# Fourth recurrent head in the wide form, memory's rows normalised in two parts, and two changes to how three streams of work are interleaved

## The chip, the cores and the metric

The kernel runs on one core of a Trainium2 chip. The metric is the device time of one execution in microseconds (us); less is better. The engines are named as in the profile: PE (TensorE matmul), PEld (its weight load), DVE (VectorE), ACT (ScalarE), POOL (GpSimd) and SP (SyncE, which here only issues DMAs). Each runs its own queue of instructions in order, and the engines wait for each other by semaphores.

## What is computed

One encoder layer over 512 tokens of width 1024, in float32. The part that the change touches is the first of three sub-layers. One input projection feeds an attention group of 8 heads and a recurrent group of 4 heads; both results go through one output projection, and then follow a cross-attention into 256 memory tokens and a gated MLP. Of the recurrent group the reference says, cut to its core:

```python
def step(S, xs):                      # chunks of tokens, both directions
    qx, kx, vx, lx = xs
    bcum = jnp.cumsum(lx, axis=-2)
    dec = jnp.exp(jnp.where(tri, bcum[..., :, None, :] - bcum[..., None, :, :], -jnp.inf))
    a = jnp.einsum("...tk,...sk,...tsk->...ts", qx, kx, dec)
    o_intra = jnp.einsum("...ts,...sv->...tv", a, vx)
    o_inter = jnp.einsum("...tk,...kv->...tv", qx * jnp.exp(bcum), S)
    ...
m = rmsnorm(mem, mem_norm_g[l])       # the memory's rows, 256 x 1024
```

## The kernel before

**Shapes.** Every large product is written as three matmuls of rounded float32 (`mm3`, lines 296 to 298: high part by high, high by low, low by high). A unit of weights is 128x1024; ACT rounds it to its high part (L240), and DVE, ACT or POOL make the low part (L242, L247, L245 with a DMA, L248). The eight PSUM banks are four tags, "b", "s", "c" and "o", of two banks each.

**The recurrent heads.** `hgrn_in(h)` projects queries and both directions' forget gates. `hgrn_core(h)` then builds a 512x512 matrix of decayed products level by level, where a level m joins neighbouring blocks of m tokens: ACT copies the keys of a level in order (L682), PE makes four 128x128 products in bank "c" (L685), DVE multiplies queries and keys by the next decay (two L711, one L716) and writes the level's products into the matrix under a mask (L725, a predicated copy). Levels 1 to 64 are done so; 128 and 256 follow with L692, L697 (transposes), L702 (the states' products) and L731 to L733 (the outputs), then ACT sums the squares (L737), POOL makes the root, DVE scales (L745), PE turns the result (L749), and ACT and DVE split it (L143, L144).

**Two forms for the diagonal and level 1.** In the narrow form (head 3, the fourth) ACT makes two copies (L669), PE makes two times four 128x128 float32 products (L672 for the diagonal, L685 with `m == 1`), ACT copies the first into the matrix (L673) and DVE puts the second in under a mask. In the wide form (heads 0 to 2) DVE multiplies queries and keys token by token (L655, L661), both results are split (L139 on ACT, L140 on DVE), and four 128x512 matmuls against a 0/1 matrix `parity` (L722) sum them, after which ACT copies the result (L723).

**How the order of the work is set.** The program is written by interleaved Python generators. `weave` (lines 83 to 105) holds a progress for each stream, as a share of the stream's total, and lets the one that is furthest behind emit its next piece; a piece says how much it counts. `pace(us)` makes a stream yield nothing until the streams together have emitted so many counted us. Nothing waits by `pace` on the chip: it only sets where instructions stand in each engine's queue. A stream that yields nothing keeps its old progress, unless it is listed in `late`:

```python
if step is None and s[0] in late and i + 1 < len(live):
    s[1] = max(s[1], live[i + 1][1] / live[i + 1][2] * s[2])
```

There are two weaves. The first (line 890) runs the projections beside the heads' cores, with `late=(cores,)`. The second (line 996) runs what is left of the cores, `attention()` and `attention_filler()`, without `late`. The attention does 32 steps i: two score matmuls (L921), a softmax (DVE maximum L899, ACT exponential L902, DVE reciprocal L903, a scaling on ACT L907 or DVE L909), four transposes of step i-2 (L931, split by L139 and L140), and every fourth step eight matmuls with the values (L942, then L946 and L947). The filler is the memory's key projection (128x256 matmuls, 192 of them), the first half of its value projection (48 matmuls of 128x512) and the first half of the output projection (96 of 128x512), whose parts after the first wait for all four recurrent heads.

**The memory's rows.** `mem_norm()` (line 844) normalises two blocks of 128 rows between head 1's and head 2's projections: a square on ACT (L344), a root on POOL, two scalings on DVE (L328) for each block.

Of the kernel before, what the change touches and what calls it, by code (L numbers as in the profile page):

```python
# [10 lines left out]
F32R = mybir.dt.float32r  # L11
# [36 lines left out]
NEG_SCALAR = frozenset(range(9, 33))  # L48
NEG_POOL = frozenset(range(33, 42))
CORE_SHARE, ATT_LEAD = 53.0, 4.0  # L50
CORE_WIDE, CORE_END = 8.0, 4.5
KEY_TURNS = {1: (0, 1), 2: (2, 3)}
WARM, SPREAD_STEP = 4, 2
LEVELS = (1, 2, 4, 8, 16, 32, 64)
# [53 lines left out]
def layer(tc, io, out):  # L108
# [23 lines left out]
    def tmp2(shape=(P, 512), dt=F32, tag="ta"):  # L132
        return t2.tile(list(shape), dt, name="tmp2", tag=tag, bufs=TMP_BUFS[tag])

    def tmp4(shape, dt=F32):
        return t4.tile(shape, dt, name="tmp4", tag="tmp4")
# [419 lines left out]
        for b in range(NB):  # L556
            put_v(b, v_ps[b])

    masks = const.tile([P, len(LEVELS), P], U8, name="masks")
    masks_f = tmp4([P, len(LEVELS), P])  # L560
# [4 lines left out]
    with tc.issue_after(last_load[0]):  # L565
        nc.sync.dma_start(lbt, io["hg_lb"])
        nc.sync.dma_start(og, io["hg_out_norm_g"][:, None])
        nc.sync.dma_start(masks_f, io["masks"])
        nc.sync.dma_start(qkg[:, 0, :], rows_bc(io["q_norm_g"], 64))
        nc.sync.dma_start(qkg[:, 1, :], rows_bc(io["k_norm_g"], 64))  # L570
        nc.sync.dma_start(cw, io["conv"])
# [68 lines left out]
    def hgrn_core(h):  # L640
# [6 lines left out]
        kt = room[:, 1024:1536].rearrange("p (s n) -> p s n", s=NB)  # L647
        st = room[:, 1536:1792].rearrange("p (g n) -> p g n", g=2)
        diag = a[:, :, 0, :]
        wide = h < 3  # L650
        near = room[:, 1024:2048]
        ksum = tmp2(tag="th")
        nc.scalar.mul(ksum, qk[:, 1, 0, :], oml[:, 0, h:h + 1])
        if wide:
            nc.vector.tensor_tensor(out=pat(near, T, [[2, T // 2], [1 - T, 2]]), in0=pat(qk, 0, [[2, T // 2], [T + 1, 2]]),  # L655
                                    in1=pat(qk, 3 * T + 1, [[2, T // 2], [-(T + 1), 2]]), op=ALU.mult)
        nc.vector.scalar_tensor_tensor(out=ksum, in0=qk[:, 1, 1, :], scalar=oml[:, 1, h:h + 1], in1=ksum,
                                       op0=ALU.mult, op1=ALU.add)
        if wide:
            pairs = lambda t: t.rearrange("p (i two) -> p i two", two=2)  # L660
            nc.vector.tensor_tensor(out=pat(near, 0, [[2, T // 2], [T + 1, 2]]), in0=pairs(ksum), in1=pairs(q),  # L661
                                    op=ALU.mult)
            sides = [[tmp2(dt=F32R, tag="th") for _ in range(2)] for _ in range(2)]
            for n in range(2):
                split(*sides[n], near[:, n * T:n * T + T])
        else:
            kc, qc = [tmp2(tag="th") for _ in range(2)]
            for side, to in ((1, kc), (0, qc)):
                nc.scalar.copy(to, pat(qk, side * 2 * T, [[2, T // 2], [T + 1, 2]]))  # L669
            o = bank("c").rearrange("p (b n) -> p b n", b=NB)  # L670
            for b in range(NB):
                nc.tensor.matmul(o[:, b, :], ksum[:, blk(b)], q[:, blk(b)], start=True, stop=True)  # L672
            nc.scalar.copy(diag, o)  # L673
            yield 1.0
        toff = 0
        for i, m in enumerate(LEVELS + (128, 256)):
            if m == 1 and wide:
                pass
            elif m <= 64:
                if m > 1:  # L680
                    kc = tmp2(tag="th")
                    nc.scalar.copy(kc, pat(qk, 2 * T, [[2 * m, T // (2 * m)], [T + m, 2], [1, m]]))  # L682
                o = bank("c").rearrange("p (b n) -> p b n", b=NB)
                for b in range(NB):
                    nc.tensor.matmul(o[:, b, :], kc[:, blk(b)], qc[:, blk(b)] if m == 1 else  # L685
                                     pat(qk, b * P, [[2 * m, P // (2 * m)], [T + m, 2], [1, m]]),
                                     start=True, stop=True)
            elif m == 128:
                o = bank("c").rearrange("p (b n) -> p b n", b=NB)
                for sb in range(NB):  # L690
                    tb = sb ^ 1
                    nc.tensor.matmul(o[:, sb, :], qk[:, 1, sb % 2, blk(sb)], qk[:, 0, tb % 2, blk(tb)],  # L692
                                     start=True, stop=True)
            else:
# [18 lines left out]
            if m < 128:  # L713
                src = tt[:, toff:toff + 2 * nblk].rearrange("p (i two) -> p two i", two=2)
                toff += 2 * nblk
                nc.vector.tensor_mul(tt[:, toff:toff + nblk], src[:, 0, :], src[:, 1, :])  # L716
                if m == 1 and wide:
                    yield from pace(CORE_WIDE)
                    o = bank("c")
                    for n in range(2):  # L720
                        for k in range(2):
                            nc.tensor.matmul(o, parity[:, n:n + P], sides[n][k], start=n + k == 0, stop=n + k == 2)  # L722
                    nc.scalar.copy(diag, o.rearrange("p (b n) -> p b n", b=NB))  # L723
                else:
                    nc.vector.copy_predicated(diag, masks[:, i:i + 1, :].to_broadcast([P, NB, P]), o)  # L725
            else:
                nc.scalar.copy(a[:, :, 1, :], o)
            yield 1.0
# [11 lines left out]
        if wide:  # L740
# [100 lines left out]
        for b in range(MB):  # L841
            nc.scalar.dma_start(kv["rows"][:, b, :], io["mem"][blk(b), :])

    def mem_norm():
        for b in range(MB):
            m = kv["rows"][:, b, :]
            r = row_rstd(m, tmp4([P, D]))
            for c in range(2):
                scale_rows(m, r, kv["g"], m, c)

    def mem_turn(b):
        if b == 0:
# [3 lines left out]
    def mix_projections():  # L856
# [541 lines left out]
```

## Time and profile before

| what | value |
|---|---|
| median of 3 runs | 814.66 us (813.87 to 815.19) |
| the profiled execution's own time | 814.31 us |
| its span, first to last instruction | 812.5 us |
| PE busy | 800.7 us, 99% |
| PE's share of the chain that ended last | 89% |
| PEld busy | 688.4 us, 85% |
| DVE busy | 582.7 us, 72% |
| ACT busy | 482.0 us, 59% |
| POOL busy | 136.5 us, 17% |

Busy time of PE counts from a matmul's start to its modelled end, and the next one starts before that, so the spans of consecutive matmuls overlap: a PE that is busy all the time can still start its matmuls later than it could. The distance from one start to the next tells more. The waits of an engine are put down to the instruction whose semaphore came last.

### The profile page before, as it was taken

The numbers are of one execution on the slowest core, as the hardware profiler recorded it, in microseconds if no ns is written. First come the engines' busy times: TensorE is split into PE (matmuls) and PEld (weight loads), VectorE is DVE, ScalarE is ACT, GpSimd is POOL, SyncE is SP. The second block draws the span as 40 slices with busy tenths as digits, with TensorE's granted clock in tenths as the row PEclk, the third lists the DMA queues.
The fourth block names the chain that finished last, engine by engine and source line by source line (L and its number), as shares of the span: only waits on it lengthen the run. The fifth ranks groups of instructions, "written<-read, shape, count | busy, mean of one in ns | idle before, by whom it ended". The sixth has DMA issues, their size and how long they took to land.

```text
span 812.5 us, 11696 instructions
## 1 busy us (share of the span) xinstructions
PE 800.7 (99%) x4390; PEld 688.4 (85%) x4390; DVE 582.7 (72%) x878; ACT 482.0 (59%) x797; POOL 136.5 (17%) x213
## 2 busy tenths in 40 slices
PE   9999999999999999999999999999999999999996
PEld 7888878899988888888888898899999998888885
DVE  5467576698896765855453767987777788888765
ACT  6675774677978873645443553665555545566651
POOL 0111201334213102301011311211111111000301
PEclk9999999999999999999999999999999999999999
DMA  8596666679777752256634158776765667278842
GB/s 300 198 267 164 137 148 130 146 187 267 206 193 191 186 188 109 86 173 170 167 117 143 33 165 205 161 199 164 187 166 141 160 187 179 91 211 277 241 127 104
DMA packets 42458, 139.61 MB, mean 172 GB/s; under 512 B 5281, under 2 KB 6561, under 8 KB 42401
## 3 DMA queue, kind: packets, MB, share of 16 engines
q1 hardware_dynamic: 28944, 97.43, 35.0%
q0 software_dynamic: 12160, 38.54, 26.8%
q10 hardware_dynamic: 1296, 2.89, 1.0%
q8 instruction: 34, 0.56, 0.3%
q14 instruction: 24, 0.19, 0.1%
HBM read 135.17 MB, written 25.17 MB: 197 GB/s over the span
## 4 chain that ended last, share of the span: by engine, by line
PE 89%; DVE 4%; ACT 4%; issue 1%; DMA 1%; POOL 1%; SPq 0%; DVEq 0%; POOLq 0%
PE ps_b L298 9%; PE ps_b L297 9%; PE ps_b L296 9%; PE ps_s L296 7%; PE ps_s L298 7%; PE ps_s L297 7%; PE ps_o L296 5%; PE ps_o L298 5%; PE ps_o L297 5%; PE ps_c L296 4%; PE ps_c L298 4%; PE ps_c L297 4%; PE ps_c L685 2%; PE ps_o L942 1%; PE ps_o L931 1%; PE ps_s L921 1%
## 5 line engine op out<-in xcount | busy, mean ns | idle before, releaser
L240 ACT CAST wh<-raw 128x1024 fp32r<-128x1024 f32 x110 | 113.8, 1036 | 106.9 <-PE ps_b L297 30.2
L242 DVE TENSOR_TENSOR wl<-raw,wh 128x1024 fp32r<-128x1024 f32 (+1 forms) x77 | 92.9, 1209 | 72.5 <-ACT wh L240 72.4
L296 PE MATMUL ps_b<-big,wh 128*128 128x512 f32 (+1 forms) x344 | 122.2, 355 | 0.0
L298 PE MATMUL ps_b<-big,wl 128*128 128x512 f32 (+1 forms) x344 | 120.9, 351 | 0.0
L297 PE MATMUL ps_b<-big,wh 128*128 128x512 f32 (+1 forms) x344 | 120.4, 350 | 0.0
L298 PEld LDWEIGHTS ps_b<-big,wl 128*128 128x128 f32 x344 | 65.0, 189 | 8.7
L297 PEld LDWEIGHTS ps_b<-big,wh 128*128 128x128 f32 x344 | 65.1, 189 | 8.2
L296 PEld LDWEIGHTS ps_b<-big,wh 128*128 128x128 f32 x344 | 65.1, 189 | 8.0
L711 DVE TENSOR_TENSOR big<-big 128x512 f32<-128x512 f32 x64 | 48.3, 769 | 9.2 <-ACT tmp L682 4.8
L296 PE MATMUL ps_s<-wh,big 128*128 128x512 f32 (+1 forms) x140 | 53.5, 383 | 0.1
L297 PE MATMUL ps_s<-wl,big 128*128 128x512 f32 (+1 forms) x140 | 53.2, 380 | 0.0
L298 PE MATMUL ps_s<-wh,big 128*128 128x512 f32 (+1 forms) x140 | 53.0, 379 | 0.0
L248 POOL DMA_DIRECT2D wl<-in_w_dram x33 | 29.4, 890 | 118.7 <-ACT wl L247 105.6
L140 DVE TENSOR_TENSOR big<-ps_o,big 128x512 fp32r<-128x512 f32 x54 | 36.8, 686 | 11.5 <-ACT big L139 11.3
L139 ACT CAST big<-ps_o 128x512 fp32r<-128x512 f32 x54 | 31.8, 589 | 17.0 <-PE ps_o L1047 7.5
L296 PE MATMUL ps_s<-big,wh 128*128 128x256 f32 (+1 forms) x120 | 40.0, 333 | 0.0
L297 PE MATMUL ps_s<-big,wh 128*128 128x256 f32 (+1 forms) x120 | 39.9, 333 | 0.0
L298 PE MATMUL ps_s<-big,wl 128*128 128x256 f32 (+1 forms) x120 | 39.9, 332 | 0.0
L297 PE MATMUL ps_c<-big,wh 128*128 128x256 f32 (+1 forms) x120 | 39.1, 325 | 0.0
L296 PE MATMUL ps_c<-big,wh 128*128 128x256 f32 (+1 forms) x120 | 39.1, 325 | 0.0
L298 PE MATMUL ps_c<-big,wl 128*128 128x256 f32 (+1 forms) x120 | 39.0, 325 | 0.0
L296 PE MATMUL ps_o<-wh,big 128*128 128x512 f32 (+1 forms) x102 | 38.8, 380 | 0.0
(322 smaller groups left out, 2147.1 us busy)
## 6 DMA issues: line engine op xcount, KB each, us to landing
raw<-in_w_dram SPq DMA_DIRECT2D x91, 512.0 KB, 3.4
wl<-in_w_dram POOLq DMA_DIRECT2D x33, 512.0 KB, 6.8
sum_t<-in_wd_dram SPq DMA_DIRECT2D x20, 512.0 KB, 6.0
tmp<-in_wu_dram SPq DMA_DIRECT2D x14, 512.0 KB, 7.3
sum_t<-in_wd_dram POOLq DMA_DIRECT2D x10, 512.0 KB, 8.1
sum_t<-sum_t POOLq DMA_DIRECT2D x10, 512.0 KB, 7.4
big<-sum_t SPq DMA_DIRECT2D x10, 512.0 KB, 4.9
raw<-sum_t SPq DMA_DIRECT2D x10, 512.0 KB, 3.8
```

What stands on the lines that cost most here:

```text
L139: nc.scalar.copy(hi, src)
L140: (eng or nc.vector).tensor_sub(lo, src, hi.bitcast(F32))
L240: nc.scalar.copy(wh, raw)
L242: last_low[0] = nc.vector.tensor_sub(wl[:, :by_dma], raw[:, :by_dma], wh[:, :by_dma].bitcast(F32)).ins
L248: nc.gpsimd.dma_start(wl[:, by_dma:], source(i)[:, by_dma:], accum_op=ALU.add)
L296: nc.tensor.matmul(o, a[0], b[0], start=start, stop=False, skip_group_check=again)
L297: nc.tensor.matmul(o, a[0], b[1], start=False, stop=False, skip_group_check=again)
L298: last_mm[0] = nc.tensor.matmul(o, a[1], b[0], start=False, stop=stop, skip_group_check=again).ins
L685: nc.tensor.matmul(o[:, b, :], kc[:, blk(b)], qc[:, blk(b)] if m == 1 else pat(qk, b * P, [[2 * m, P // (2 * m)], [T + m, 2], [1, m]]), st ...
L711: nc.vector.tensor_tensor(out=c, in0=c, in1=pat(tt, toff + off, [[2, npair], [gap, 2], [0, m]]), op=ALU.mult)
L921: nc.tensor.matmul(s, qT[h // 4][:, h % 4, blk(qb)], kT[:, 2 * (h // 4) + c, :], start=c == 0, stop=c == 1)
L931: nc.tensor.transpose(o[:, c, :], e[:, 0, blk(c)], ident)
```

## The change

Five edits. (1) `wide = h < 3` goes: head 3 takes the wide form too, and with it the two paces that only wide heads had, `CORE_WIDE` before the `parity` matmuls and `CORE_END` before the last scaling. (2) The mask of level 1 is no longer loaded or converted (six masks and not seven). (3) `pace(CORE_COPY)`, 1.2 us of counted work, stands between the transposes of level 256 and the states' products, in every head. (4) `mem_norm` takes one block: block 0 where both stood, block 1 after the first projection of head 2. (5) The second weave gets `late=(cores,)`.

```diff
-CORE_WIDE, CORE_END = 8.0, 4.5
+CORE_WIDE, CORE_COPY, CORE_END = 8.0, 1.2, 4.5
...
-        nc.sync.dma_start(masks_f, io["masks"])
+        nc.sync.dma_start(masks_f, io["masks"][:, 1:, :])
...
-        wide = h < 3
...
-        else:
-            kc, qc = [tmp2(tag="th") for _ in range(2)]
-            for side, to in ((1, kc), (0, qc)):
-                nc.scalar.copy(to, pat(qk, side * 2 * T, [[2, T // 2], [T + 1, 2]]))
-            o = bank("c").rearrange("p (b n) -> p b n", b=NB)
-            for b in range(NB):
-                nc.tensor.matmul(o[:, b, :], ksum[:, blk(b)], q[:, blk(b)], start=True, stop=True)
-            nc.scalar.copy(diag, o)
-            yield 1.0
...
                 nc.scalar.copy(kt, o)
                 yield 0.5
+                yield from pace(CORE_COPY)
                 o = bank("c")[:, :256].rearrange("p (g n) -> p g n", g=2)
...
-                if m == 1 and wide:
+                if m == 1:
                     yield from pace(CORE_WIDE)
...
-        if wide:
-            yield from pace(CORE_END)
+        yield from pace(CORE_END)
...
-        mem_norm()
+        mem_norm(0)
         nothing = lambda: None
-        yield from hgrn_in(2, [nothing] * 3 + [lambda: mem_turn(0), nothing, nothing, lambda: mem_turn(1)])
+        yield from hgrn_in(2, [lambda: mem_norm(1), nothing, nothing, lambda: mem_turn(0), nothing, nothing,
+                               lambda: mem_turn(1)])
...
-    weave((cores, 34.0), (attention(), 46.0), (attention_filler(), 52.0))
+    weave((cores, 34.0), (attention(), 46.0), (attention_filler(), 52.0), late=(cores,))
```

What this does to the queues is shown at three places. In the changed program the line numbers are its own: L905 is L921 of before, L915 is L931, L926 is L942, L733 is L749, L669 is L685, L707 is L722, L883 is L899, L887 is L903, L893 is L909, L931 (on DVE) is L947, L696 is L711 and L710 is L725.

**Head 3's first products on PE.** Before, behind the turn of head 2's result (`ps_c<-ident`):

```order
L749 MATMUL ps_c<-ident,tmp_1868 128x128 x4
L672 MATMUL ps_c<-tmp_1296,tmp_2045 128x128 x4
L921 MATMUL ps_s<-big 128x512 x4
L685 MATMUL ps_c<-tmp_2049,tmp_2048 128x128 x4
L685 MATMUL ps_c<-big,tmp_2135 128x128 x4
```

In the change, 35 rows further down the same queue:

```order
L707 MATMUL ps_c<-tmp_2081,parity 128x512
L298 MATMUL ps_b<-big,wl 128x256
L296 MATMUL ps_b<-big,wh 128x256
L707 MATMUL ps_c<-tmp_2082,parity 128x512
L297 MATMUL ps_b<-big,wh 128x256
L298 MATMUL ps_b<-big,wl 128x256
L296 MATMUL ps_b<-big,wh 128x256
L297 MATMUL ps_b<-big,wh 128x256
L669 MATMUL ps_c<-big,tmp_2263 128x128
```

The first level's products stood at once behind the turn; they now stand after the second score, with 46 of the filler's 128x256 matmuls between the turn and the third score, some of them in between the products.

**DVE in the attention, between two row maxima.** Before, from the maximum of step 8 (whose row comes just above the first of these) to that of step 9:

```order
L140 TENSOR_TENSOR big<-ps_o,big 128x4x128
L903 RECIPROCAL small<-small 128x1
L711 TENSOR_TENSOR big<-big 128x16x2x16
L947 TENSOR_TENSOR tmp_2186<-ps_o,tmp_2186 64x512
L140 TENSOR_TENSOR big<-ps_b,big 128x256
L140 TENSOR_TENSOR big<-ps_o,big 128x4x128
L711 TENSOR_TENSOR big<-big 128x32x2x8
L725 COPY_PREDICATED big<-masks,ps_c 128x4x128
L903 RECIPROCAL small<-small 128x1
L140 TENSOR_TENSOR big<-ps_o,big 128x4x128
L909 TENSOR_SCALAR tmp_2277<-tmp_2277,small 128x512
L140 TENSOR_TENSOR big<-ps_b,big 128x256
```

and then one more L711, one more L725 and the maximum. In the change, the longest such stretch, from step 9's maximum to those of steps 10 and 11:

```order
L140 TENSOR_TENSOR big<-ps_o,big 128x4x128
L931 TENSOR_TENSOR tmp_2199<-ps_o,tmp_2199 64x512
L696 TENSOR_TENSOR big<-big 128x32x2x8 x2
L140 TENSOR_TENSOR big<-ps_o,big 128x4x128
L887 RECIPROCAL small<-small 128x1
L710 COPY_PREDICATED big<-masks,ps_c 128x4x128
L893 TENSOR_SCALAR tmp_2244<-tmp_2244,small 128x512
L140 TENSOR_TENSOR big<-ps_o,big 128x4x128
L887 RECIPROCAL small<-small 128x1
L140 TENSOR_TENSOR big<-ps_o,big 128x4x128
L883 TENSOR_REDUCE small<-ps_s 128x1 x2
```

One level's work stands there and not two half levels, and the levels are spread over more steps of the attention: the last product of head 3's levels (L692) stands ahead of step 13's score before, and ahead of step 17's in the change.

**PE late in the attention.** Before, a step of the plain pattern:

```order
L921 MATMUL ps_s<-big 128x512 x2
L931 MATMUL ps_o<-ident,tmp_2682 128x128 x4
L296 MATMUL ps_b<-wh,big 128x512
L297 MATMUL ps_b<-wl,big 128x512
L298 MATMUL ps_b<-wh,big 128x512
```

(the last three twice) and in the change, from step 21's score on:

```order
L905 MATMUL ps_s<-big 128x512 x2
L915 MATMUL ps_o<-ident,tmp_2697 128x128 x4
L905 MATMUL ps_s<-big 128x512 x2
L733 MATMUL ps_c<-ident,tmp_2738 128x128
L296 MATMUL ps_b<-wh,big 128x512
L297 MATMUL ps_b<-wl,big 128x512
L298 MATMUL ps_b<-wh,big 128x512
L915 MATMUL ps_o<-ident,tmp_2752 128x128 x4
L296 MATMUL ps_b<-wh,big 128x512
L297 MATMUL ps_b<-wl,big 128x512
L298 MATMUL ps_b<-wh,big 128x512
L926 MATMUL ps_o<-big,vv 128x512 x8
```

Between the scores of steps 20 and 28 stand 23 of the filler's matmuls and not 48, because the value projection is used up and the output projection's next part waits for head 3, whose turn (L733) now stands behind step 22's score and not behind step 19's. The 25 others follow, with more, in one block of 31 ahead of step 29's score.

## Rows read from the trace of the kernel before

**Rows 1.** Windows: stretch, length; busy of PE, PEld, DVE, ACT, POOL; granted clock; DMA.

```profile
207.20:256.40 49.20, 47.97 (x328) 42.02 (x327) 42.60 (x82) 41.27 (x84) 12.12 (x13) 1.00 0.78 204
256.40:299.00 42.60, 42.60 (x221) 34.83 (x220) 31.94 (x64) 35.14 (x76) 7.01 (x8) 1.00 0.67 169
```

**Rows 2.** Chain that ended last, 205 to 300 us: start, length, engine, tile, line.

```profile
213.03 1.40 ACT tmp L907 x2
...
232.16 1.13 PE ps_c L685 x8
...
247.30 0.66 PE ps_o L931 x4
```

**Rows 3.** PE's groups by line, 207.4 to 256.4 us: count, busy, mean ns, idle.

```profile
L921 PE MATMUL ps_s<-big 128*128 128x512 f32 x32 | 10.8, 419 | 0.2 <-ACT tmp L902 0.2
L931 PE MATMUL ps_o<-ident,tmp 128*128 128x128 f32 x56 | 8.7, 278 | 0.6 <-DVE big L140 0.3 <-ACT tmp L907 0.2
L296 PE MATMUL ps_b<-big,wh 128*128 128x256 f32 x28 | 8.5, 303 | 0.0
...
L685 PE MATMUL ps_c<-big,tmp 128*128 128x128 f32 x48 | 6.8, 282 | 0.4 <-DVE big L711 0.4
L942 PE MATMUL ps_o<-big,vv 128*128 128x512 f32 x24 | 6.1, 395 | 0.0
L296 PE MATMUL ps_b<-wh,big 128*128 128x512 f32 x6 | 2.6, 440 | 0.0
```

**Rows 4.** PE in order of time: start, length, line, operation, count.

```profile
108.33 1.08 PE L722 MATMUL ps_c<-tmp,parity 128*128 128x512 f32 x4
109.25 0.39 PE L296 MATMUL ps_b<-big,wh 128*128 128x512 f32 x1
...
207.66 1.06 PE L672 MATMUL ps_c<-tmp,tmp 128*128 128x128 f32 x8
208.47 1.17 PE L921 MATMUL ps_s<-big 128*128 128x512 f32 x4
209.47 1.07 PE L685 MATMUL ps_c<-tmp,tmp 128*128 128x128 f32 x8
210.38 1.12 PE L685 MATMUL ps_c<-big,tmp 128*128 128x128 f32 x8
...
229.78 0.28 PE L297 MATMUL ps_b<-big,wh 128*128 128x256 f32 x1
229.90 0.28 PE L298 MATMUL ps_b<-big,wl 128*128 128x256 f32 x1
...
256.95 0.60 PE L931 MATMUL ps_o<-ident,tmp 128*128 128x128 f32 x4
257.31 0.48 PE L296 MATMUL ps_b<-wh,big 128*128 128x512 f32 x1
...
258.79 0.62 PE L921 MATMUL ps_s<-big 128*128 128x512 f32 x2
...
261.07 0.63 PE L921 MATMUL ps_s<-big 128*128 128x512 f32 x2
```

**Rows 5.** The score of step 9 on PE, and later its maximum on DVE.

```profile
226.10 0.71 PE L921 MATMUL ps_s<-big 128*128 128x512 f32 x2
...
232.55 0.67 DVE L899 TENSOR_REDUCE small<-ps_s 128x1 f32<-128x512 f32 x1
233.15 0.67 DVE L140 TENSOR_TENSOR big<-ps_o,big 128x512 fp32r<-128x512 f32 x1
```

**Rows 6.** DVE in order of time, head 1: one token-by-token product and what follows it.

```profile
98.77 1.12 DVE L655 TENSOR_TENSOR big<-big 128x512 f32<-128x512 f32 x1
99.74 0.71 DVE L144 SCALAR_TENSOR_TENSOR big<-ps_c,og,big 128x512 fp32r<-128x512 f32 x1
```

**Rows 7.** PE in order of time: two waits ahead of the attention, in brackets.

```profile
112.79 1.23 PE L685 MATMUL ps_c<-big,tmp 128*128 128x128 f32 x8 [0.87 <-ACT tmp L682]
...
195.44 1.16 PE L702 MATMUL ps_c<-big 128*128 128x128 f32 x8 [0.47 <-ACT big L698]
```

More of the change, by code (lines that the diff above doesn't have):

```diff
@@ L557, in spread_r @@
             put_v(b, v_ps[b])
-    masks = const.tile([P, len(LEVELS), P], U8, name="masks")
-    masks_f = tmp4([P, len(LEVELS), P])
+    masks = const.tile([P, len(LEVELS) - 1, P], U8, name="masks")
+    masks_f = tmp4([P, len(LEVELS) - 1, P])
     lbt = const.tile([P, 2, 2, 4], F32, name="lbt")
@@ L653, in hgrn_core @@
         nc.scalar.mul(ksum, qk[:, 1, 0, :], oml[:, 0, h:h + 1])
-        if wide:
-            nc.vector.tensor_tensor(out=pat(near, T, [[2, T // 2], [1 - T, 2]]), in0=pat(qk, 0, [[2, T // 2], [T + 1, 2]]),
-                                    in1=pat(qk, 3 * T + 1, [[2, T // 2], [-(T + 1), 2]]), op=ALU.mult)
+        nc.vector.tensor_tensor(out=pat(near, T, [[2, T // 2], [1 - T, 2]]), in0=pat(qk, 0, [[2, T // 2], [T + 1, 2]]),
+                                in1=pat(qk, 3 * T + 1, [[2, T // 2], [-(T + 1), 2]]), op=ALU.mult)
@@ L657, in hgrn_core @@
         nc.vector.scalar_tensor_tensor(out=ksum, in0=qk[:, 1, 1, :], scalar=oml[:, 1, h:h + 1], in1=ksum,
                                        op0=ALU.mult, op1=ALU.add)
[L659 to L665, printed above, removed]
-        else:
-            kc, qc = [tmp2(tag="th") for _ in range(2)]
-            for side, to in ((1, kc), (0, qc)):
-                nc.scalar.copy(to, pat(qk, side * 2 * T, [[2, T // 2], [T + 1, 2]]))
-            o = bank("c").rearrange("p (b n) -> p b n", b=NB)
-            for b in range(NB):
-                nc.tensor.matmul(o[:, b, :], ksum[:, blk(b)], q[:, blk(b)], start=True, stop=True)
-            nc.scalar.copy(diag, o)
-            yield 1.0
+        pairs = lambda t: t.rearrange("p (i two) -> p i two", two=2)
@@ L675, in hgrn_core @@
+        nc.vector.tensor_tensor(out=pat(near, 0, [[2, T // 2], [T + 1, 2]]), in0=pairs(ksum), in1=pairs(q), op=ALU.mult)
+        sides = [[tmp2(dt=F32R, tag="th") for _ in range(2)] for _ in range(2)]
+        for n in range(2):
+            split(*sides[n], near[:, n * T:n * T + T])
         toff = 0
         for i, m in enumerate(LEVELS + (128, 256)):
-            if m == 1 and wide:
[L678 to L682, printed above, removed]
+            if 1 < m <= 64:
+                kc = tmp2(tag="th")
+                nc.scalar.copy(kc, pat(qk, 2 * T, [[2 * m, T // (2 * m)], [T + m, 2], [1, m]]))
@@ L683, in hgrn_core @@
                 o = bank("c").rearrange("p (b n) -> p b n", b=NB)
                 for b in range(NB):
-                    nc.tensor.matmul(o[:, b, :], kc[:, blk(b)], qc[:, blk(b)] if m == 1 else
+                    nc.tensor.matmul(o[:, b, :], kc[:, blk(b)],
                                      pat(qk, b * P, [[2 * m, P // (2 * m)], [T + m, 2], [1, m]]),
@@ L693, in hgrn_core @@
                                      start=True, stop=True)
-            else:
+            elif m == 256:
                 o = bank("c").rearrange("p (b n) -> p b n", b=NB)
@@ L716, in hgrn_core @@
                 nc.vector.tensor_mul(tt[:, toff:toff + nblk], src[:, 0, :], src[:, 1, :])
-                if m == 1 and wide:
+                if m == 1:
                     yield from pace(CORE_WIDE)
@@ L724, in hgrn_core @@
                 else:
-                    nc.vector.copy_predicated(diag, masks[:, i:i + 1, :].to_broadcast([P, NB, P]), o)
+                    nc.vector.copy_predicated(diag, masks[:, i - 1:i, :].to_broadcast([P, NB, P]), o)
             else:
@@ L739, in hgrn_core @@
         yield 3.0
-        if wide:
-            yield from pace(CORE_END)
+        yield from pace(CORE_END)
         while len(sg_box) < 1 + NB:
@@ L842, in mem_load, with mem_norm @@
             nc.scalar.dma_start(kv["rows"][:, b, :], io["mem"][blk(b), :])
[L844 to L849, printed above, removed]
+    def mem_norm(b):
+        m = kv["rows"][:, b, :]
+        r = row_rstd(m, tmp4([P, D]))
+        for c in range(2):
+            scale_rows(m, r, kv["g"], m, c)
     def mem_turn(b):
```

## Prediction, made before the changed kernel was run

> **What bounds the kernel now.** The page comes first: PE is busy 99% of the span and carries 89% of the chain that ended last, so anything taken off PE, or any hole in PE's queue that closes, comes off the time, and work on other engines counts only where PE waits for it. The change touches PE's queue in earnest only where head 3 runs beside the attention, so I read the windows of that part next: from 207.2 us, where head 2's result is turned, to 256.4, where the plain pattern of the attention begins, and from there to 299.0 [rows 1]. PE is busy for 47.97 of the 49.20 us of the first stretch, and for all of the second. The first stretch looks nearly full. The chain of waits says otherwise: between 213 and 247 us it runs through ACT and DVE (the scalings, the level products L711, the splits) and passes through PE only at 232.16, until it is back on PE at 247.30 [rows 2]. So I counted what PE has to do in the first stretch and compared it with the clock on the wall.
>
> The counts are in the groups by line [rows 3], the prices are distances from one start to the next [rows 4]. A 128x512 matmul takes 0.23 us (four in 0.92, 108.33 to 109.25), a 128x256 one 0.12 (229.78 to 229.90), a record of a 128x128 float32 product 0.108 (sixteen in 0.81 + 0.91), a transpose 0.09 (four in 0.36, 256.95 to 257.31). There are 32 + 24 + 18 = 74 of the first (the 18 are three lines of 6), 84 of the second (three lines of 28), 48 + 56 = 104 of the third (the 56 are L672, the first L685, L692, L702 and L731 to L733), and 56 + 8 = 64 transposes: 17.0 + 10.1 + 11.2 + 5.8 = 44.1 us. A plain step of the attention (two scores, four transposes, six filler matmuls) is 2.20 by the same prices and takes 2.28 [rows 4], so hand-overs cost 0.08 a step, 1.3 us for 16 steps. That leaves 49.2 - 44.1 - 1.3 = **3.8 us that PE loses** in the first stretch. One place shows how: the score of step 9 starts on PE at 226.10, its maximum starts on DVE at 232.55 [rows 5], behind the level work of head 3.
>
> The busy row alone would put the loss at 49.20 - 47.97 = 1.2 us [rows 1]. The Trainium skill (Perfetto Trace Analysis, Identifying the Most-Contended Engine) calls matmul busy time a poor measure, because matmuls are pipelined, and wants the share of weight loads instead. The rows agree as far as they go: PEld is busy 42.02 of 49.20 us, 85%, in a stretch where PE shows 98%. With 1.2 us as all that can be won from waits, the sum below would end near 813.3.
>
> **The change, part by part.**
>
> *Head 3 in the wide form, on PE.* L672 and the first L685 go: 0.81 + 0.91 = 1.72 us. Four 128x512 matmuls come: 0.92 [rows 4]. PE is the bound, so -0.8 us.
>
> *The same, on the other engines.* ACT loses two copies and gets two casts of the same shape, and copies one bank as before: nothing. DVE gets two token-by-token products of 0.97 us each [rows 6] and two subtractions at 0.60 (the distance behind the maximum, rows 5), and loses a masked copy of about that length: some 2.5 us more. That would cost nothing only where DVE has room: it is busy 42.60 of 49.20 us here [rows 1]. In the new order these 2.5 us stand at the very start, where PE now has 46 filler matmuls of 0.12, 5.5 us, between the turn of head 2 and the third score; I take them as covered there, and keep the 2.5 us for a rival.
>
> *Waiting counts as progress (and the two paces of a wide head).* This moves most. No instruction is added; the levels of head 3 are spread. Before, L692, the end of its levels, stood ahead of step 13's score, now ahead of step 17's. Four more steps bring PE 55 matmuls of 128x512 and 16 transposes more, 12 of 128x256 and 16 records less: 12.7 + 1.4 - 1.4 - 1.7 = 11.0 us. They bring DVE four steps' work at 31.94/16 = 2.0 us [rows 1] and the 2.5: 10.5. By this, DVE's lead over PE shrinks by only 0.4 us, and so might the loss. The other end is that all 3.8 us go: the longest run of DVE work between two maxima falls from 14 instructions to 11, and the row maxima are what frees the score banks, so PE may not wait at all. I take 2.0 of the 3.8, near the middle, since the rows favour neither end.
>
> *What is late next.* Between the scores of steps 20 and 28 PE has 23 filler matmuls and not 48. Its work there is 16 + 16 + 23 matmuls of 128x512 and 36 transposes, 12.7 + 3.2 = 15.9, with hand-overs 16.5 us. ACT at 35.14/16 = 2.2 us a step [rows 1] has 17.6, DVE 16.0. So ACT could hold PE back by 1.0 us; at best by nothing, as part of those 2.2 us is weight casting for filler that now stands later. I take 0.6. The 31 filler matmuls that follow are 7.1 us of PE work for which nothing has to be ready but weights, so what ACT and DVE are behind by then is made up and not passed on. Weights are cast three units ahead, as before.
>
> *Pace ahead of the states' products.* For heads 0 and 1 it puts six matmuls between the copy L698 and the products L702, where the list of PE's waits has no wait; for head 2, the one place with such a wait (0.47 us at 195.44 [rows 7]), the order of PE is unchanged; for head 3 none was there. Bounds 0 and -0.5; I take 0.
>
> *Memory's rows in two parts.* In the new order the squares on ACT still stand side by side, one scaling on DVE moves behind a projection's scaling, and one weight pass (L247) moves behind three gate functions. The nearest wait of PE is 0.87 us at 112.79 [rows 7], more than twenty us later, behind ACT work whose order is the same. Bounds 0 and -0.9; I take 0.
>
> *One mask less.* A transfer and a conversion on POOL become one seventh shorter, once, long before the first masked copy; POOL is 17% busy. Nothing.
>
> Sum: -0.8 - 2.0 + 0.6 = -2.2 us. The profiled execution took 814.31, so its like would take 812.1; that execution lies 0.35 under the median of the runs, 814.66. Against the median: **812.5 us**.
>
> **The rivals.** What a measurement of this kernel can tell from no change is 0.2%, 1.6 us: under 813.0 is faster, over 816.3 slower.
>
> *The waits only move.* DVE keeps its lead and PE waits as long in the new places, so that only the 0.8 us on PE count, less up to 0.6: 813.9 to 814.5. For it: the 0.4 us above. Against it: the chain leaves PE exactly where head 3's levels and the softmaxes meet, and these are thinned out.
>
> *DVE carries the stretch.* If the stretch is held by DVE's queue and not by single waits, its 2.5 us come on top and what PE saves is worth nothing: 814.66 + 2.5 = 817.2, slower. It decides from the point where DVE has no idle time left up to L692; the 5.5 us of filler at the start speak against it. The same page of the Trainium skill says that the engine with the highest occupancy is the most contended and to be relieved first, PE judged by its weight loads. By that rule DVE (87%) leads PEld (85%) in this stretch, and the change loads it further; the chain [rows 2] agrees with the rule.
>
> *The thin steps starve PE.* If a step between the scores 20 and 28 cannot be shorter than a plain one, because scores, exponential, scaling and transposes wait for each other in a ring of two banks, eight of them take 8 x 2.28 and two turns of L942 at 8 x 0.23, 21.9 us and not 16.5: 5.4 us, and 814.66 - 0.8 - 2.0 + 5.4 = 817.3. It turns the whole change slower from 4.4 us on. For it: the thin order. Against it: no engine's work fills more than 17.6 us there.
>
> *More goes.* The 0.87 us at 112.79 and the 0.47 at 195.44 vanish too, with the forecast: 811.1.
>
> **How the numbers follow.** Forecast 0.58 (its own range: -0.8 - 3.8 = 810.1 to -0.8 - 0.4 + 1.0 = 814.5; under 813.0 in 0.54); waits only move 0.24; DVE carries 0.06; thin steps 0.06; more goes 0.06. Faster: 0.54 + 0.06 = 0.60; slower: 0.06 + 0.06 = 0.12; the same: 0.28. The range leaves out the two slow rivals and the best tail: 810.3 to 814.9.
>
> **What would show it.** In the changed profile, counted as above: the first score to the start of the plain steps should lose about 1.8 us and not 3.8; the maximum of each step should start within 3 us of its score (step 9: 6.4 before); four L707 and no L672 should stand on PE; waits between scores 20 and 28 should stay under 1 us; the waits at 112.79 and 195.44 should still be there. It is wrong if PE's loss up to L692 is as long as before, if ACT or DVE shows no idle time between steps 20 and 28 while PE waits, or if the part before 205 us changes by over 0.5 us.

## The result, and the profile after

The changed kernel takes **816.05 us** (median of 21 runs, 815.39 to 818.55) against 814.31 us of the kernel before (21 runs beside it): a ratio of 1.0023, 95% interval 1.0017 to 1.0030. The forecast was 812.5 us; the change is slower by 1.7 us. That is clear of zero, but the interval's lower end, 1.0017, still lies within the 0.2% that the prediction counts as no change. The profiled execution spans 814.6 us, 2.1 more than that of before. Two lines of the page:

```profile
span 814.6 us, 11677 instructions
PE 801.7 (98%) x4378; PEld 687.3 (84%) x4378; DVE 584.9 (72%) x881; ACT 480.9 (59%) x797; POOL 137.6 (17%) x213
```

The windows of the changed kernel (stretch, length; busy of PE, PEld, DVE, ACT, POOL; granted clock; DMA). The first two answer to [rows 1]:

```profile
207.20:256.40 49.20, 47.29 (x302) 40.24 (x300) 44.90 (x83) 41.18 (x82) 14.86 (x15) 1.00 0.81 216
256.40:299.00 42.60, 42.56 (x231) 34.58 (x230) 33.58 (x69) 35.45 (x79) 5.11 (x6) 1.00 0.52 136
...
208.00:220.00 12.00, 11.41 (x83) 10.52 (x83) 10.28 (x16) 8.56 (x15) 5.97 (x6) 1.00 1.04 262
...
250.00:260.00 10.00, 9.17 (x54) 6.93 (x54) 9.80 (x18) 7.69 (x15) 2.19 (x3) 1.00 1.00 261
```

The last two stretches in the kernel before:

```profile
208.00:220.00 12.00, 11.87 (x88) 10.83 (x87) 10.90 (x24) 11.32 (x23) 1.66 (x2) 1.00 0.86 223
...
250.00:260.00 10.00, 10.00 (x68) 8.90 (x67) 5.33 (x11) 7.69 (x21) 3.15 (x4) 1.00 0.69 171
```

Between 207 and 256 us PE now gets through 302 records (entries of the trace; a 128x128 float32 product has two) and not 328; 12 of the 26 are taken out by the change itself. Between 250 and 260 us DVE is busy for 9.80 of 10 us, where it was busy for 5.33, and PE stands for 0.83 us that it did not stand before.

**Where the 2.1 us are.** As in the prediction, but with prices read a little finer, every distance from one start on PE to the next is compared with the price of the first one's shape in an unbroken row (0.226 us for 128x512, 0.120 for 128x256, 0.111 for a 128x128 product, 0.108 for a transpose); what is over is called PE's loss, and it is summed over three parts: up to the memory's first key matmul after 200 us, from there to the first matmul behind the attention, and the rest. Work (the sum of prices) falls by 0.87 us (190.24 + 94.76 against 189.88 + 94.25). The loss grows from 8.51 to 8.92 in the first part, **from 4.80 to 6.92 in the attention**, and from 4.00 to 4.45 behind it, where 0.36 is a single wait for a weight transfer at 554.5 us. 0.41 + 2.12 + 0.45 - 0.87 = 2.1. The two outer parts are less certain than the middle one: traces of kernels that hardly differ there are as far apart. Of the experiments below, e_late and x_delay have neither the third nor the fourth edit, and their first part loses 8.88 and 9.30 us; the last part loses 3.7 to 4.8 us over all of them.

The places are PE's waits in the changed kernel (start, length; in brackets the idle time before it and what ended it; the loss by starts is somewhat longer than that idle time):

```profile
113.39 1.23 PE L669 MATMUL ps_c<-big,tmp 128*128 128x128 f32 x8 [1.26 <-ACT tmp L666]
...
215.56 0.50 PE L707 MATMUL ps_c<-tmp,parity 128*128 128x512 f32 x1 [0.47 <-DVE tmp L140]
...
229.31 2.08 PE L926 MATMUL ps_o<-big,vv 128*128 128x512 f32 x8 [0.29 <-DVE small L887]
...
252.17 0.73 PE L905 MATMUL ps_s<-big 128*128 128x512 f32 x2 [0.35 <-ACT tmp L886]
...
255.40 1.16 PE L676 MATMUL ps_c<-big 128*128 128x128 f32 x8 [0.47 <-DVE big L696]
```

The first answers to [rows 7]: 0.87 has become 1.26. The second is new: the second parity product of head 3 waits for DVE's split, and 1.21 us are lost ahead of the third score (0.10 before). The third, ahead of products with the values, waits for a reciprocal of a softmax. The last two lie ahead of the scores of the steps 14 to 18, where the levels of head 3 now stand and where 0.45 + 0.43 + 0.62 + 1.06 + 0.44 = 3.0 us are lost.

There the row maxima are late as well. The maximum of step 16, whose score is the fourth of the rows above, starts 6.4 us behind that score:

```profile
258.57 0.68 DVE L883 TENSOR_REDUCE small<-ps_s 128x1 f32<-128x512 f32 x1
```

In the kernel before, only the maxima of the steps 9, 10 and 13 start more than 3 us behind their scores (6.4, 4.5 and 3.2 us); in the changed kernel those of the steps 0, 1, 13 to 16 and 20 do (4.4 to 6.4 us). The score of step 16 itself waits for an exponential (L886), which follows such a late maximum.

**Why DVE is late.** DVE in order of time in the kernel before, around the turn of head 2:

```profile
203.53 0.74 DVE L657 SCALAR_TENSOR_TENSOR tmp<-big,oml,tmp 128x512 f32<-128x512 f32 x1
204.19 0.42 DVE L140 TENSOR_TENSOR big<-ps_b,big 128x256 fp32r<-128x256 f32 x1
204.52 2.13 DVE L711 TENSOR_TENSOR big<-big 128x512 f32<-128x512 f32 x2
207.69 0.42 DVE L140 TENSOR_TENSOR big<-ps_b,big 128x256 fp32r<-128x256 f32 x1 [1.04 <-ACT big L139]
208.58 0.75 DVE L144 SCALAR_TENSOR_TENSOR big<-ps_c,og,big 128x512 fp32r<-128x512 f32 x1 [0.46 <-ACT big L143]
```

and in the changed kernel:

```profile
204.03 0.74 DVE L655 SCALAR_TENSOR_TENSOR tmp<-big,oml,tmp 128x512 f32<-128x512 f32 x1
204.69 0.42 DVE L140 TENSOR_TENSOR big<-ps_b,big 128x256 fp32r<-128x256 f32 x1
207.69 0.42 DVE L140 TENSOR_TENSOR big<-ps_b,big 128x256 fp32r<-128x256 f32 x1 [2.59 <-ACT big L139]
208.03 1.52 DVE L653 TENSOR_TENSOR big<-big 128x512 f32<-128x512 f32 x1
210.57 0.42 DVE L140 TENSOR_TENSOR big<-ps_b,big 128x256 fp32r<-128x256 f32 x1 [1.02 <-ACT big L139]
211.16 0.75 DVE L144 SCALAR_TENSOR_TENSOR big<-ps_c,og,big 128x512 fp32r<-128x512 f32 x1 [0.17 <-ACT big L143]
211.83 1.10 DVE L658 TENSOR_TENSOR big<-tmp,tmp 128x512 f32<-128x512 f32 x1
212.76 2.23 DVE L696 TENSOR_TENSOR big<-big 128x512 f32<-128x512 f32 x2
214.81 0.69 DVE L140 TENSOR_TENSOR tmp<-big,tmp 128x512 fp32r<-128x512 f32 x1
215.42 0.68 DVE L883 TENSOR_REDUCE small<-ps_s 128x1 f32<-128x512 f32 x1
216.01 0.93 DVE L140 TENSOR_TENSOR tmp<-big,tmp 128x512 fp32r<-128x512 f32 x1
```

Before, the two scalings of level 1 (L711, 2.13 us) fill an idle stretch of DVE at 204.5 us. In the wide form they must follow the token-by-token products (L653, L658), because the scalings overwrite what the products read, and the first product stands behind two splits of the memory's keys (L140). So DVE idles for 2.59 and 1.02 us, and all of head 3's start (two products, two scalings, two subtractions, some 6.5 us) is done from 208 us on, when the softmaxes need DVE as well. The first product writes into head 3's `room` (L645), which in the changed program lies where head 2's `room`, with its matrix, lay (the expectations below take it for the buffer of head 2's queries and keys). Its last reader, L718 on PE, is done at 200.3 us, so by 208 the memory has long been free; late is the product's place in DVE's queue. Whether the reuse of this buffer sets that place, or the amount of work costs wherever it stands, is what the later experiments test.

### The profile page after: what moved, and what is told of

The parts are those of the page before. It is cut to its first block, busy times and chain, and to the rows that moved or that the text cites. A ratio compares the mean times of both kernels' runs of the same rounds, so it can differ in the third digit from the quotient of the medians.

```text
span 814.6 us, 11677 instructions
## 1 busy us (share of the span) xinstructions
PE 801.7 (98%) x4378; PEld 687.3 (84%) x4378; DVE 584.9 (72%) x881; ACT 480.9 (59%) x797; POOL 137.6 (17%) x213
## 5 line engine op out<-in xcount | busy, mean ns | idle before, releaser
L696 DVE TENSOR_TENSOR big<-big 128x512 f32<-128x512 f32 x64 | 48.5, 773 | 8.7 <-ACT tmp L666 4.2
L140 DVE TENSOR_TENSOR big<-ps_o,big 128x512 fp32r<-128x512 f32 x54 | 36.9, 685 | 12.2 <-ACT big L139 10.7
```

What stands on the lines that cost most here:

```text
L140: (eng or nc.vector).tensor_sub(lo, src, hi.bitcast(F32))
L696: nc.vector.tensor_tensor(out=c, in0=c, in1=pat(tt, toff + off, [[2, npair], [gap, 2], [0, m]]), op=ALU.mult)
```

## The experiments

**The edits one at a time.** Alone on the kernel before: the fifth edit; the first two; the third and fourth. And all but the fifth.

```diff
# e_late, the kernel before with the fifth edit
-    weave((cores, 34.0), (attention(), 46.0), (attention_filler(), 52.0))
+    weave((cores, 34.0), (attention(), 46.0), (attention_filler(), 52.0), late=(cores,))
# e_wide, the changed kernel without the third, fourth and fifth
-                yield from pace(CORE_COPY)
...
         mem_norm(0)
+        mem_norm(1)
...
-        yield from hgrn_in(2, [lambda: mem_norm(1), nothing, nothing, lambda: mem_turn(0), nothing, nothing,
-                               lambda: mem_turn(1)])
+        yield from hgrn_in(2, [nothing] * 3 + [lambda: mem_turn(0), nothing, nothing, lambda: mem_turn(1)])
...
-    weave((cores, 34.0), (attention(), 46.0), (attention_filler(), 52.0), late=(cores,))
+    weave((cores, 34.0), (attention(), 46.0), (attention_filler(), 52.0))
# e_small, the kernel before with the third and fourth edit as in the change
# e_no_late, the changed kernel, the last two lines of e_wide alone
```

> The kernel before with the fifth edit alone: waiting counts as progress in the second weave, head 3 stays narrow. Theory A (three small causes: the wide form's start on DVE, the spread levels, and the first part, where PE's wait at 112 us grew from 0.87 to 1.26 us): the spread levels cost 0.8 us, 815.1 against 814.3. Theory B (the spread of the levels is the whole cause): 1.2 us or more, 815.5 and above. Theory C (only the wide form and the spread together cost something): no more than the kernel before, 813.3 to 814.3, since the maxima are freed earlier.

Measured: 813.65 against 814.67, ratio **0.9986** (0.9978 to 0.9995), loss in the attention 3.50 (4.80 before). The fifth edit gains 1.1 us. Of the three theories only C had it no slower than the kernel before, and C falls with the next run.

> The kernel before with head 3 in the wide form (and one mask less, and its two paces) alone. Theory A: PE's work falls by 0.9 us and a wait of 1.2 us comes where its second parity product waits for DVE's split: 814.6 against 814.3. Theory B: the wide form gives what it takes off PE, 0.9 us: 813.4. Theory C: 813.4 to 814.

Measured: 817.6, ratio **1.0038** (1.0026 to 1.0050), loss in the attention 8.59. Worse than all three theories: the wide form costs 3.1 us where it was to give 0.9.

> The kernel before with the two edits of the first part alone: the pace ahead of the states' products, and memory's rows in two parts. Theory A: L702's move by six matmuls makes ACT late by 0.6 us and PE's wait at 112 us grows by 0.4: 814.7 against 814.3. Theories B and C: nothing, within 0.2 us of 814.3, and the wait at 112 us as long as before in the profile.

Measured: 815.53, ratio 1.0006 (0.9995 to 1.0016); PE's wait at 113.52 us is 1.25 us. As theory A had it for the wait; in time it is within the noise.

> The changed kernel without the fifth edit: edits 1 to 4 stay. Theory A: 0.3 for the wide form and 0.4 for the first part, 815.0. Theory B: 813.4, faster than the kernel before by the 0.9 us that PE has less to do. Theory C: 813.4 to 814.3.

Measured: 817.73, ratio 1.0039 (1.0026 to 1.0052), loss in the attention 8.48. With the wide form in, the fifth edit still saves 1.3 us (1.0039 against 1.0023). The two intervals overlap, but the loss in the attention says the same (8.48 against 6.92). Theories A to C fall: the loss is the wide form's, and the fifth edit hides part of it.

**What of the wide form costs.** The changed kernel without it; its delay alone, and its work alone, put into the narrow form with the fifth edit; and the wide form without its delay.

```diff
# e_no_wide, the kernel before with the third, fourth and fifth edit
# x_delay, e_late's kernel
             nc.scalar.copy(diag, o)
             yield 1.0
+            yield from pace(CORE_WIDE)
...
# x_dve, e_late's kernel: the products of L655 and L661 for all heads, and for head 3
...
+            for n in range(2):
+                nc.vector.tensor_tensor(out=near[:, n * T:n * T + T], in0=near[:, n * T:n * T + T],
+                                        in1=qk[:, 0, n, :], op=ALU.subtract)
# x_wide_now, the changed kernel
-                    yield from pace(CORE_WIDE)
+                    yield from pace(CORE_WIDE if h < 3 else 0.0)
```

> The changed kernel without the wide form of head 3 (edits 3, 4 and 5 stay, seven masks). Theory D (the wide form's work on DVE costs) and theory P (its pace costs) both want the time of the fifth edit alone plus what the first part's edits cost, 813.65 + 0.9 = 814.5, about the time of the kernel before. If the wide form were not the part that loses, it would be near the changed kernel's 816.

Measured: 812.57 against 815.58, ratio **0.9965** (0.9952 to 0.9977), loss in the attention 2.72. The wide form is the part that loses; without it the rest of the change is faster than the kernel before, and by more than was expected.

> The kernel before with the fifth edit, head 3 narrow, and the pace of 8 us of a wide head put into it between the diagonal and level 1: the delay of the wide form without its work. Theory P (head 3's levels come later by the pace and meet the dense steps): 2 us or more above the fifth edit alone, 815.7 and above. Theory D: within 0.5 us of it, 813.2 to 814.2.

Measured: 814.84, ratio 0.9996 (0.9987 to 1.0005), 0.8 us over the fifth edit alone (0.9986). The intervals overlap; the loss in the attention is 4.79 against 3.50. Between the two theories.

> The kernel before with the fifth edit, head 3 narrow, and the wide form's four extra operations on DVE (two token-by-token products, two subtractions; their result is not used) put at its start: its work without its delay. Theory D: 2 to 3 us above the fifth edit alone, 815.7 to 816.7. Theory P: less than 0.7 us above it, 813.6 to 814.3.

Measured: 818.7, ratio 1.0038 (1.0025 to 1.0052), 4.2 us over the fifth edit alone, loss in the attention 8.60. Theory D, and more than it asked: four operations that take 1.76 + 1.10 + 1.26 = 4.1 us in its trace cost 4.2. Part of this is not the work's own: the first product takes 1.76 us here and 1.12 to 1.16 in the other heads, because POOL makes a weight's low part beside it, from 208.74 to 210.02 us (see the last section).

> The changed kernel with the pace ahead of the parity products taken out for head 3 alone (the other three heads keep it), so that its levels start 8 us of counted work earlier. Theory P: 2 us below the changed kernel, 814.0. Theory D: within 0.7 us of the changed kernel, 815.4 to 816.8, with PE waiting for DVE's splits at the start in place of later.

Measured: 814.72, ratio 0.9995 (0.9985 to 1.0005), 2.3 us under the changed kernel. Theory P had this one. So neither is alone: the work costs most, and with it the delay costs 2.3 us, against 0.8 without it. The loss ahead of the third score stays (1.23); that ahead of the scores of the steps 14 to 18 falls from 3.0 to 1.2 (0.24 + 0.12 + 0.49 + 0.10 + 0.29).

**Work or place.** The changed kernel with the token-by-token products in a buffer of their own (y_near); the same without the pace of x_wide_now (y_near_now); x_dve with that buffer (z_dve).

```diff
-        near = room[:, 1024:2048]
+        near = tmp4([P, 1024]) if h == 3 else room[:, 1024:2048]
```

> The changed kernel, but the token-by-token products of head 3 go to a buffer of their own, so that they need not wait for the buffer of head 2's queries and keys and stand ahead of head 2's turn on DVE. Theory place (the wide form costs because its DVE work stands at 208 to 217 us, behind an idle stretch of DVE): 2 us or more under the changed kernel, a ratio to the kernel before of 1.000 or less, and no PE wait of over 0.5 us ahead of the third score. Theory amount (3 us more of DVE work cost wherever they stand): within 0.7 us of the changed kernel, a ratio of 1.0015 to 1.003.

Measured: ratio 1.0004 (0.9989 to 1.0019), 1.5 us under the changed kernel by the ratios, though the two intervals touch; the loss ahead of the third score is 0.24 (1.21), that in the attention 5.65 (6.92). The wait came out as theory place has it; the time lies between the two theories, nearer to place.

> The same, and the pace ahead of head 3's parity products taken out. Theory place: the two gains add, 2 us under the version without that pace alone (ratio 0.9995), so 0.997. Theory amount: 0.9995 as that one.

Measured: 812.92 against 814.76, ratio **0.9983** (0.9974 to 0.9992), loss in the attention 3.40. The time lies between the two theories (0.997 and 0.9995). This version has the five edits, but without the pace ahead of head 3's parity products; it is 3.3 us under the changed kernel and 1.4 under the kernel before by the ratios. On its DVE the first product stands at 182.0 us and not at 208.0:

```profile
182.01 1.15 DVE L653 TENSOR_TENSOR tmp<-big 128x512 f32<-128x512 f32 x1
...
204.44 0.74 DVE L655 SCALAR_TENSOR_TENSOR tmp<-big,oml,tmp 128x512 f32<-128x512 f32 x1
...
205.22 1.13 DVE L658 TENSOR_TENSOR tmp<-tmp,tmp 128x512 f32<-128x512 f32 x1
206.19 0.42 DVE L140 TENSOR_TENSOR big<-ps_b,big 128x256 fp32r<-128x256 f32 x1
206.53 1.15 DVE L696 TENSOR_TENSOR big<-big 128x512 f32<-128x512 f32 x1
...
207.56 0.68 DVE L140 TENSOR_TENSOR tmp<-tmp,tmp 128x512 fp32r<-128x512 f32 x1
208.16 0.41 DVE L140 TENSOR_TENSOR big<-ps_b,big 128x256 fp32r<-128x256 f32 x1
210.34 0.69 DVE L140 TENSOR_TENSOR tmp<-tmp,tmp 128x512 fp32r<-128x512 f32 x1 [1.77 <-PE ps_c L733]
```

The second product, a scaling and the first subtraction are done in the stretch in which DVE idled.

> The kernel before with the fifth edit, head 3 narrow, with the wide form's four extra DVE operations (result not used), as once already, but writing to a buffer of their own and so standing earlier on DVE. Theory place: most of the 4.2 us by which that work slowed the kernel goes, a ratio to the kernel before of 0.9985 to 1.000. Theory amount: still 3 us or more over the fifth edit alone, 1.002 or more.

Measured: 815.36, ratio 1.0007 (0.9997 to 1.0016); 2.5 of the 4.2 us go, and 1.7 stay over the fifth edit alone. Between the two theories: the place is the larger part, the amount the smaller. Of the amount's part some is again POOL's: one scaling takes 2.03 us at 207.99, beside POOL's low part from 207.71.

**The first part's edits.** The changed kernel without the third (e_no_copy), and without the fourth edit (e_no_mem), by the lines of e_wide above.

> The changed kernel without the pace ahead of the states' products. If that pace made ACT late in the first part (it moves the states' products of head 0 by six matmuls, and the squares of memory's rows queue behind what follows them), the wait at 112 us is 0.87 us again and not 1.26, and the time falls by 0.4 us. If the split of memory's rows did it, the wait stays at 1.26.

> The changed kernel with memory's rows normalised in one part as before. If the split made ACT late, the wait at 112 us is 0.87 us again and the time falls by 0.4 us; if the pace ahead of the states' products did it, the wait stays at 1.26 us.

PE's wait without the third edit:

```profile
112.86 1.23 PE L669 MATMUL ps_c<-big,tmp 128*128 128x128 f32 x8 [0.94 <-ACT tmp L666]
```

and without the fourth:

```profile
114.62 1.23 PE L669 MATMUL ps_c<-big,tmp 128*128 128x128 f32 x8 [1.31 <-ACT tmp L666]
```

The pace makes the wait longer; the split of memory's rows does not. All 18 traces agree: the wait is 1.25 to 1.31 us in the eight kernels with the pace in heads 0 to 2 and 0.87 to 0.94 in the ten without. The times miss: 1.0029 (1.0019 to 1.0040) without the third edit and 1.0024 (1.0015 to 1.0033) without the fourth. Why the first of these is no faster stays open. Its trace, of an execution of 815.59 us where the median is 817.83, loses 2.60 us ahead of the third score (1.21), but over the whole attention 6.96 (6.92).

How six matmuls ahead of the states' products reach a wait 27 us later is seen on ACT, before:

```profile
86.36 1.07 ACT L344 ACTIVATE tmp<-big 128x1024 f32<-128x1024 f32 x1
...
89.22 1.05 ACT L240 CAST wh<-raw 128x1024 fp32r<-128x1024 f32 x1 [0.66 <-PE ps_b L297]
...
94.66 1.05 ACT L240 CAST wh<-raw 128x1024 fp32r<-128x1024 f32 x1 [0.50 <-PE ps_b L297]
```

and in the changed kernel:

```profile
87.96 1.07 ACT L344 ACTIVATE tmp<-big 128x1024 f32<-128x1024 f32 x1
...
90.04 1.06 ACT L240 CAST wh<-raw 128x1024 fp32r<-128x1024 f32 x1
...
95.28 1.03 ACT L240 CAST wh<-raw 128x1024 fp32r<-128x1024 f32 x1
```

Head 0's last output product starts 1.6 us later on PE (86.52 and 84.93), and with it come its squares and, behind these on ACT, memory's squares (L344). The two idle times of ACT, 0.66 and 0.50 us, take up 1.0 of it; 0.6 us of delay is left, goes on from cast to gate to copy, and lengthens PE's wait by 0.39 us.

**With the place mended, wide or narrow, late or not.** The own buffer, no pace ahead of the parity products, the pace of the third edit for head 3 alone; the same with head 3 narrow (without the buffer); the same wide without the fifth edit.

```diff
# z_wide, y_near_now's kernel; z_narrow, e_no_wide's kernel; z_wide_no_late, z_wide's without late=(cores,)
-                yield from pace(CORE_COPY)
+                yield from pace(CORE_COPY if h == 3 else 0.0)
```

> The changed kernel with the own buffer for head 3's products, without the pace ahead of its parity products, and with the pace ahead of the states' products for head 3 alone. Both theories: 0.3 to 0.4 us under the version that keeps that pace in all heads (ratio 0.9983), so 0.998, with the wait at 112 us back at 0.9 us. Theory place: no slower than z_narrow on the same chip, up to 0.9 us faster, as PE has that much less to do. Theory amount: 0.5 us or more slower than z_narrow.

> The changed kernel with head 3 narrow, and the pace ahead of the states' products for head 3 alone: 0.4 us under the version that keeps that pace in all heads (ratio 0.9965 on a noisy chip, 2.7 us of PE lost in the attention), so 0.996 to 0.9975, with the wait at 112 us back at 0.9 us.

> z_wide without the fifth edit. If waiting counted as progress is what spreads head 3's levels to the good whatever its form, it is 1 us or more slower than z_wide, 0.9992 or more; if that edit only made good for the wide form's place, about equal to z_wide.

Measured on one chip: wide 0.9991 (0.9982 to 1.0000), narrow 0.9986 (0.9977 to 0.9995), wide without the fifth edit 0.9990 (0.9981 to 0.9999). PE's wait at 112 us is 0.92 and 0.88 us, as expected, but the times did not get the 0.3 us: 0.998 was expected of the wide version, 0.9975 at most of the narrow one. With the place mended, no gain of the wide form over the narrow one shows. By the ratios it is 0.4 us slower, well within the noise, so theories place (up to 0.9 us faster) and amount (0.5 or more slower) are not told apart here. In the attention the wide version's trace gives back 0.41 of the 0.87 us of PE work (loss 3.83 against 3.42); the rest goes in the outer parts, which differ between traces anyway. The fifth edit is then worth nothing that shows in the time, and 0.57 us in the loss (4.40 against 3.83). So what it saves depends on what else stands in head 3's order.

## Why the prediction was wrong

- **Head 3 wide, on PE: -0.8.** Right: the work of PE falls by 0.87 us.
- **The same on DVE: "I take them as covered there".** This is the step that failed. The 46 filler matmuls are cover for PE; the step asked whether PE had other work, not whether DVE could start its own. In DVE's order the first product stands behind splits that wait for the same filler, DVE idles for 3.6 us, and the level 1 scalings, which had used that idle time, are pushed behind it as well. So not 2.5 but 6.5 us of DVE work land between 208 and 217 us: the two scalings, and 4.2 us of products and subtractions, which the prediction priced at 3.1. The sign of the whole change is here: the first two edits alone cost 3.1 us, and a buffer of their own for the two products takes 1.5 us of the changed kernel's time away. The place is not all: the same work put into a good place of the narrow form still costs 1.7 us (z_dve), so "covered" fails for the amount too.
- **Waits: -2.0 of 3.8.** The fifth edit does what this term said, to about half: alone it takes the attention's loss from 4.80 to 3.50 and 1.1 us off the time. In the changed kernel the levels come later by the wide form's pace and with more behind them in DVE's queue, and 3.0 us are lost ahead of the scores of the steps 14 to 18. From the first score to the plain steps (step 16 before, step 18 after) PE loses 5.5 us by the prices used here and 4.0 before, where the prediction wanted 1.8 and 3.8. The term was worked out from the number of DVE operations between two maxima, as if the levels would move without a backlog.
- **Thin steps: +0.6.** Right: 1.0 us is lost between the scores 20 and 28 against 0.5 before, and the rival of 5.4 us is out.
- **The pace ahead of the states' products: "Bounds 0 and -0.5; I take 0".** Wrong in sign for the wait it touches, which is 0.39 us longer; in the time the two first-part edits show nothing clear of the noise (e_small, 1.0006). No loss was allowed for since PE does not wait there; but what is moved back on PE is what ACT's queue waits for.
- **Memory's rows in two parts: 0.** Borne out by its wait. **One mask less** was not tried alone.
- **The rivals.** "DVE carries the stretch", given 0.06, named the right engine, with another mechanism and price: the 0.87 us on PE do count, and the loss in the attention grows by 2.1 us. It was to decide "from the point where DVE has no idle time left up to L692"; DVE did have 3.6 us left, and could not use it. The Trainium skill's rule that the prediction set beside this rival (Perfetto Trace Analysis, Identifying the Most-Contended Engine) calls the engine with the highest occupancy the most contended. The trace agrees: DVE goes from 42.60 to 44.90 of 49.20 us there, PEld from 42.02 to 40.24. The chain, which the prediction took as agreeing, did not single DVE out: read whole, from 213.0 to 247.3 us, it has 15.25 us on ACT and 12.64 on DVE. "The waits only move", given 0.24, came true of the late maxima, but they grew in moving, and its 813.9 to 814.5 did not come.
- **The signs.** Four parity products did replace L672, and the loss between the scores 20 and 28 stayed at 1.0 us, the most that was allowed. Step 9's maximum starts 0.66 us behind its score (231.22 and 231.88), but the sign was meant for every step, and seven maxima are over 3 us late. PE's loss up to L692, which was to show the forecast wrong if it stayed as long, is longer. Row maxima still hold PE in part, beside the splits and level scalings.

**Open:** why the version without the wide form measured 0.9965 while z_narrow, which differs in the pace of heads 0 to 2 alone, measured 0.9986 on another chip. By its wait z_narrow should have been the faster, and in the two profiled executions it is (spans of 811.0 and 811.4 us), so the two chips may be the cause; the two kernels were not run on one chip. Not tried alone were the pace `CORE_END` that came with the wide form, and the mask.

## What to carry to other kernels

Work added to a second engine is covered only if that engine can start it: look in its own order at what stands in front, and whether a reused buffer or an in-place update ties it there, before setting its length against the other engine's work. A pace or wait that costs its own engine nothing can be paid by the engine that waits for its result; follow the result's queue to the next place where it has no idle time left. And test an edit that spreads work together with and without the edits that load the same engine: here the fifth edit was worth 1.1 to 1.3 us, or nothing that shows.

## What the runs showed of the hardware

Of the 64 level scalings on DVE in the changed kernel's trace (both inputs in SBUF), 54 take 0.67 to 0.70 us and eight of level 1 take 1.16 to 1.20. The other two take 1.54 and 1.53: they began just after POOL had begun to make a weight's low part. One of them, on DVE and then on POOL:

```profile
253.81 1.53 DVE L696 TENSOR_TENSOR big<-big 128x512 f32<-128x512 f32 x1
```

```profile
253.77 1.04 POOL L245 TENSOR_SCALAR wl<-wh 128x1024 fp32r<-128x1024 f32 x1 [3.50 <-ACT wh L240]
```

POOL started 0.04 us earlier, and DVE took 0.85 us more; PE's wait ahead of L676 at 255.40 is for this scaling. In the kernel before the same happens at 236.57 (1.44 us, against POOL's 236.43 to 237.47). Where DVE began first, it kept its time and POOL was the slower: 0.68 us on DVE at 234.28, 1.43 on POOL from 234.44, in place of 1.04. Head 3's first product (1.52 us at 208.03, 1.13 to 1.17 in the other heads) also ran into POOL, from 207.49 to 208.54. The Trainium skill (Trainium Architecture — The Big Picture, What this means for kernel authors) says that DVE and GpSimd contend for a shared port pair by an exclusive lock; the rows agree. In this kernel it costs PE 0.47 us in one place.
